# Two mixers of a transformer kernel: gates, branch products and gated sum computed with tokens on the partitions and 512 weight columns streamed

## The chip, the core and the metric

The kernel runs on one core of one Trainium2 chip. The metric is the device time of one execution in microseconds (us); smaller is better. Engines are named as the profile names them: PE is TensorE's matmul, PEld its weight load, DVE is VectorE, ACT is ScalarE, POOL is GpSimd, SP issues the DMAs.

## What is computed

256 tokens of width 1024 pass ten sublayers: two layers of (half a swiglu, first mixer, half a swiglu), then two layers of (second mixer, swiglu). The change touches the ends of the mixers alone, where gated branches are summed and projected:

```python
# first mixer: o_a, o_b, o_c are attention outputs [256, 512]
merged = (sigmoid(ga) * (o_a @ w_br_a)       # ga, gb, gc: [256, 1024] of x @ w_in
          + sigmoid(gb) * (o_b @ w_br_b)     # w_br_*: [512, 1024]
          + sigmoid(gc) * (o_c @ w_br_c))
x = layer_norm(ALPHA * x + merged @ w_out)   # w_out: [1024, 1024]

# second mixer: a [256, 512], conv [256, 256], pooled groups d [256, 4, 64]
merged = g0 * (a @ w_attn_out) + g1 * (conv @ w_conv_out) + g2 * (d @ w_grp) * scale
x = x + merged @ w_o                         # followed by an rmsnorm
```

Sums are to be exact to about float32. Each float32 operand is therefore held as two float32r parts, high and low, and a product is three matmuls: high x high, high x low, low x high.

## The kernel before

Everything stays on chip except the weights. XH and XL (lines 197 and 198) hold the two parts of the transposed input of a sublayer, [128 features, 8 blocks, 256 tokens]. Weights come as slabs of 128 x 1024: `slab` (line 178) loads one by a DMA on SP's queue into one of 4 "raw" buffers, ACT writes its high part `wh` (line 175), DVE its low part `wl` (line 176), each into one of 9 slots. PSUM banks come from four tags (line 156): "acc" 3, "s" 2, "pt" 2, "tp" 1. Pages in SBUF come from tags too (line 155); "gate" and "m" have 2 each.

Two forms of product with x occur. `projects` (line 355) has tokens on the output's partitions: a block of x is the stationary operand, 512 weight columns stream, and it ends with one bank for each tile of 128 tokens (`mm3`, lines 187 to 189). `project_t` (line 369) has features on the output's partitions: a 128 x 128 block of weights is stationary and the 256 tokens stream (`mm3_t`, lines 192 to 194).

The end of a mixer is built of `gates`, `merge`, `branch`, `out_project` (lines 549 to 591), all with features on the partitions. `gates` projects 1024 gate columns in two chunks of 512 through `project_t` and takes tanh(gate / 2) on ACT. `branch` multiplies four feature pairs f2, each [2 x 128 features, 256 tokens] in one "acc" bank, over the K blocks of its weights, and `merge` adds (tanh + 1) * product into the sum M (DVE, lines 561 to 565). `out_project` splits M straight into XH and XL (line 583), loads 8 slabs, and then for each token tile t runs 48 matmuls with 512 columns into two banks and calls `finish(t, O)`. In `finish` (line 885) the result is added to x (lines 299, 300), normed (`layer_norm`, lines 303 to 310, or `rms_norm`, lines 312 to 324), transposed block by block and split into XH and XL for the next sublayer: `to_xt` (line 326) uses the bank "tp" for the first four blocks and "s" (tile 0) or "pt" (tile 1) for the other four.

Nothing in the code orders engines against each other: the framework derives the waits from the tiles, and its scheduler fixes at build time the order of instructions on each engine, by priority of the program's order among what its own model of durations holds for ready. Matmuls of a later part may so be placed into holes of an earlier one: the first gate matmuls stand among the last attention heads.

Of the kernel before, what the change touches and what calls it, by code (L numbers as in the profile page):

```python
# [20 lines left out]
HD = 64  # L21
# [3 lines left out]
# type 1 column groups of w_in  # L25
# [8 lines left out]
# column ranges of the packed constants  # L34
# [39 lines left out]
def slab_cols(w):  # L74
    """[1024, 512 n] -> [n, 4, 128, 2 * 512]: slab (chunk, quarter of K)."""
    n = w.shape[1] // 512
    return w.reshape(4, 2, 128, n, 512).transpose(3, 0, 2, 1, 4).reshape(n, 4, 128, 1024)


def slab_rows(w):  # L80
    """[128 n, 1024] -> [n, 128, 1024]."""
    return w.reshape(-1, 128, 1024)
# [7 lines left out]
def layout(inp):  # L90
    """Data layout only: the arrays as the kernel reads them."""
# [6 lines left out]
    for l in range(DEPTH):  # L98
        for n in ("ffn1", "ffn2"):
# [11 lines left out]
            slab_rows(a["w_br_a"][l]),  # L111
            slab_rows(a["w_br_b"][l].reshape(8, HD, D)[GQA_ORDER].reshape(512, D)),
            slab_rows(a["w_br_c"][l])])
# [6 lines left out]
        o[f"w2_attn_{l}"] = slab_rows(a["w_attn_out_2"][l])  # L120
        o[f"w2_conv_{l}"] = slab_rows(a["w_conv_out_2"][l])
# [22 lines left out]
def block_kernel(ctx: ExitStack, tc: tile.TileContext, I, out, stages=ALL):  # L144
# [28 lines left out]
    def split(dst_h, dst_l, src):  # L173
        """src as the sum of two float32r parts"""
        A.activation(dst_h, src, AF.Copy)  # L175
        V.tensor_sub(dst_l, src, dst_h.bitcast(F32))  # L176
# [103 lines left out]
    def rsqrt(v, n, eps):  # L280
        """(v + eps) ** -0.5"""
# [13 lines left out]
    def add_stats(t, O, c):  # L295
        """X[t] += c * O, with the statistics of the sum"""
# [29 lines left out]
    def to_xt(t, src):  # L326
        """src [128 tokens, 1024] -> the parts of its transpose in XH, XL"""
        for r in range(2):
            p = bank("tp" if r == 0 else ("s", "pt")[t])
            for k in range(4):  # L330
                T.transpose(p[:, k * 128:(k + 1) * 128],
                            src[:, (4 * r + k) * 128:(4 * r + k + 1) * 128], ident)
            sl = (slice(None), slice(4 * r, 4 * r + 4), slice(t * 128, t * 128 + 128))
            split(XH[sl], XL[sl], p.rearrange("p (k n) -> p k n", k=4))

# [19 lines left out]
    def projects(*jobs, ws=None):  # L355
        """x @ [1024, n] for each job (src, evac, n): first token tile of all, then second"""
# [12 lines left out]
    def project_t(src, evac, order=(0, 1, 2, 3)):  # L369
        """(x @ [1024, 512])^T: evac(j, psum) gets feature blocks order[2j], order[2j + 1]"""  # L370
# [86 lines left out]
    def attend(heads, o, vt, vi, pen, mult=None, sinks=None):  # L457
        """heads(h, t, psum): logits of head slot h, tile t. o [128, 2, 8, 64]."""
# [63 lines left out]
    def o_parts(o):  # L522
        """o [128, 2, 8, 64] -> parts of its transpose, [128, 4, 256] each"""
# [10 lines left out]
    def head_transposes(dst, t, src, n=4, scale=None):  # L534
        """src [128, 2n heads, 64] -> dst[:, :n, tile t], two heads on the partitions"""
# [13 lines left out]
    def gates(srcs):  # L549
        gt = [page("gate", [128, 4, S], name="gate") for _ in range(2)]  # L550
        for n in range(2):
            project_t(srcs[n], lambda j, p: A.activation(
                gt[n][:, 2 * j:2 * j + 2], pairs(p), AF.Tanh, scale=0.5))
        return gt

    def merge(gt, f2, p, M, first):
        """M (+)= (tanh(gate / 2) + 1) * p over feature blocks 2 f2, 2 f2 + 1"""
        g = gt[f2 // 2][:, (f2 % 2) * 2:(f2 % 2) * 2 + 2]
        m = M[f2 // 2][:, (f2 % 2) * 2:(f2 % 2) * 2 + 2]
        if first:  # L560
            V.scalar_tensor_tensor(m, g, 1.0, p, op0=OP.add, op1=OP.mult)
        else:
            y = tmp.tile([128, 2, S], F32, tag="ropa", bufs=2, name="gm")
# [3 lines left out]
    def branch(srcs, slabs, parts, M, first):  # L567
        gt = gates(srcs)
        w = [slab(s) for s in slabs]
        for f2 in range(4):  # L570
            p = pairs(bank("acc"))
            for i in range(2):
                c = slice((2 * f2 + i) * 128, (2 * f2 + i) * 128 + 128)
                for k, wk in enumerate(w):
                    mm3_t(p[:, i], (wk[0][:, c], wk[1][:, c]),
                          (parts[0][:, k, :], parts[1][:, k, :]), k == 0, k == len(w) - 1)
            merge(gt, f2, p, M, first)

    def out_project(src, M, finish):
        """finish(t, O) with O = M^T @ [1024, 1024]"""  # L580
        for i in range(4):
            sl = (slice(None), slice(2 * i, 2 * i + 2))
            split(XH[sl], XL[sl], M[i // 2][:, (i % 2) * 2:(i % 2) * 2 + 2])
        w = [slab(src[s]) for s in range(8)]
        for t in range(2):
            O = [bank(("s", "pt")[t]) for _ in range(2)]
# [6 lines left out]
    def new_merged():  # L593
        return [page("m", [128, 4, S], name="merged") for _ in range(2)]

# [1 line left out]
    def mixer1(l, finish):  # L597
        w = I[f"w_in_{l}"]

        def rope(p, t, v, nh):  # L600
            """p [128, nh, 64] rotated, as two terms"""
# [32 lines left out]
        # keys shared by heads: [content, content | index, index | two kv heads]  # L634
# [17 lines left out]
        # indexer scores  # L652
# [30 lines left out]
        # all but the 64 largest scores of a query get the penalty  # L683
# [18 lines left out]
        for i, parts in enumerate((oap, obp, ocp)):  # L702
            branch((w[6 + 2 * i], w[7 + 2 * i]), [I[f"w_br_{l}"][i, s] for s in range(4)], parts,
                   M, i == 0)
# [233 lines left out]
```

## Time and profile before

| | |
|---|---|
| time, median of 3 runs | 2102.02 us (2100.25 to 2103.0) |
| span of the profiled execution | 2109.7 us |
| PE busy | 2067.6 us, 98% |
| DVE busy | 1288.1 us, 61% |
| ACT busy | 944.3 us, 45% |
| DMA | 359.16 MB, mean 170 GB/s |
| mean granted clock of TensorE | 0.993 |

The span runs from the first to the last instruction of one profiled execution; the timed runs are other executions, and their median lies 7.7 us below that span. The share of busy time of PE contains modelled ends of overlapping matmuls; what a matmul costs in a dense stream is read from the distance between the starts of two neighbours in the timeline.

### The profile page before, as it was taken

The page shows a single profiled execution, that of the slowest core. Times are in us where ns is not written, and L with a number is a line of the kernel's source. Part 1 is how long each engine was busy: PE and PEld are TensorE (multiplying, and loading weights), DVE is VectorE, ACT ScalarE, POOL GpSimd, SP SyncE. Part 2 cuts the span into 40 slices and gives each one's busy share as a digit, 9 for nine tenths or more (in the row PEclk, how much of TensorE's full clock was granted, in tenths as well). Part 3 has the DMA queues.
Part 4 walks back from the last instruction along what each step waited for, and adds up shares of the span by engine and source line. Part 5 has one row for each costly group of instructions (what it writes and reads, how often), then busy time and mean ns, then how long its engine had stood idle before and what let it go on. Part 6 is the DMA issues. An engine that isn't in the chain of part 4 may idle for free.

```text
span 2109.7 us, 33644 instructions
## 1 busy us (share of the span) xinstructions
PE 2067.6 (98%) x13656; PEld 1870.0 (89%) x13656; DVE 1288.1 (61%) x2044; ACT 944.3 (45%) x1281; POOL 48.6 (2%) x64
## 2 busy tenths in 40 slices
PE   8999999999999999999999999999999989999999
PEld 7998779988998999788998998789899978997998
DVE  6657974575557555975567557555755565366554
ACT  5543554444444443545435443554344444344442
POOL 0000000000000000000000001200000020000000
PEclk9999999999999999999999999999999999899999
DMA  8654532556555554541556554535565553355552
GB/s 301 197 195 158 173 116 81 180 191 200 188 193 201 178 190 156 178 160 32 170 190 232 183 189 143 181 102 166 181 211 182 175 175 120 112 180 178 192 187 91
DMA packets 99996, 359.16 MB, mean 170 GB/s; under 512 B 11904, under 2 KB 11904, under 8 KB 99840
## 3 DMA queue, kind: packets, MB, share of 16 engines
q1 hardware_dynamic: 99840, 357.00, 50.3%
q8 instruction: 107, 1.75, 0.3%
q14 instruction: 49, 0.40, 0.1%
HBM read 355.91 MB, written 1.05 MB: 169 GB/s over the span
## 4 chain that ended last, share of the span: by engine, by line
PE 87%; DVE 4%; DMA 3%; ACT 2%; POOL 1%; issue 1%; SPq 0%; POOLq 0%; ACTq 0%; DVEq 0%
PE acc L194 16%; PE acc L192 16%; PE acc L193 16%; PE acc L188 4%; PE acc L189 4%; PE acc L187 4%; PE s L187 3%; PE s L188 3%; PE s L189 3%; PE pt L189 3%; PE pt L188 3%; PE pt L187 3%; PE s L627 2%; DVE wl L176 2%; ACT wh L175 2%; PE pt L483 1%
## 5 line engine op out<-in xcount | busy, mean ns | idle before, releaser
L176 DVE TENSOR_TENSOR wl<-raw,wh 128x1024 fp32r<-128x1024 f32 (+1 forms) x656 | 783.8, 1219 | 457.3 <-ACT wh L175 453.5
L175 ACT ACTIVATE wh<-raw 128x1024 fp32r<-128x1024 f32 (+1 forms) x656 | 667.7, 1052 | 487.4 <-PE acc L194 299.6
L192 PE MATMUL acc<-xh,wh 128*128 128x256 f32 x2624 | 745.8, 284 | 0.0
L193 PE MATMUL acc<-xh,wl 128*128 128x256 f32 x2624 | 744.7, 284 | 0.0
L194 PE MATMUL acc<-xl,wh 128*128 128x256 f32 x2624 | 744.5, 284 | 0.0
L192 PEld LDWEIGHTS acc<-xh,wh 128*128 128x128 f32 x2624 | 504.0, 192 | 3.1 <-issue 1.1
L193 PEld LDWEIGHTS acc<-xh,wl 128*128 128x128 f32 x2624 | 504.1, 192 | 1.7
L194 PEld LDWEIGHTS acc<-xl,wh 128*128 128x128 f32 x2624 | 504.1, 192 | 1.5 <-issue 1.5
L187 PE MATMUL acc<-wh,xh 128*128 128x512 f32 (+1 forms) x512 | 203.8, 398 | 7.2 <-ACT wh L175 7.1
L188 PE MATMUL acc<-wl,xh 128*128 128x512 f32 (+1 forms) x512 | 203.0, 396 | 0.5 <-DVE wl L176 0.5
L189 PE MATMUL acc<-wh,xl 128*128 128x512 f32 (+1 forms) x512 | 202.1, 395 | 0.0
L394 DVE SCALAR_TENSOR_TENSOR h<-th,acc 128x256 f32<-128x256 f32 x132 | 55.1, 417 | 169.7 <-ACT th L393 169.7
L393 ACT ACTIVATE th<-acc 128x256 f32<-128x256 f32 x132 | 49.3, 373 | 229.5 <-PE acc L194 201.5
L187 PEld LDWEIGHTS acc<-wh,xh 128*128 128x128 f32 x512 | 98.0, 191 | 27.7 <-ACT wh L175 7.1
L188 PEld LDWEIGHTS acc<-wl,xh 128*128 128x128 f32 x512 | 97.7, 191 | 20.5 <-DVE wl L176 1.5
L189 PEld LDWEIGHTS acc<-wh,xl 128*128 128x128 f32 x512 | 97.4, 190 | 19.5 <-issue 0.7
L187 PE MATMUL s<-wh,ht 128*128 128x512 f32 x264 | 103.5, 392 | 0.0
L188 PE MATMUL s<-wl,ht 128*128 128x512 f32 x264 | 103.4, 392 | 0.0
L189 PE MATMUL pt<-wh,ht 128*128 128x512 f32 x264 | 103.1, 391 | 0.0
L187 PE MATMUL pt<-wh,ht 128*128 128x512 f32 x264 | 103.0, 390 | 0.0
L188 PE MATMUL pt<-wl,ht 128*128 128x512 f32 x264 | 102.8, 389 | 0.0
L189 PE MATMUL s<-wh,ht 128*128 128x512 f32 x264 | 102.0, 389 | 0.0
(249 smaller groups left out, 2246.5 us busy)
## 6 DMA issues: line engine op xcount, KB each, us to landing
raw<-in_w_in_dram SPq DMA_DIRECT2D x184, 512.0 KB, 4.4
raw<-in_ffn_in_dram SPq DMA_DIRECT2D x176, 512.0 KB, 4.6
raw<-in_ffn_out_dram SPq DMA_DIRECT2D x88, 512.0 KB, 4.6
raw<-in_w_ffn_in_dram SPq DMA_DIRECT2D x88, 512.0 KB, 4.4
raw<-in_w_ffn_out_dram SPq DMA_DIRECT2D x44, 512.0 KB, 4.5
raw<-in_w_br_dram SPq DMA_DIRECT2D x24, 512.0 KB, 4.4
raw<-in_w_out_dram SPq DMA_DIRECT2D x16, 512.0 KB, 4.8
raw<-in_w_o_dram SPq DMA_DIRECT2D x16, 512.0 KB, 4.2
```

The source lines that it names most:

```text
L175: A.activation(dst_h, src, AF.Copy)
L176: V.tensor_sub(dst_l, src, dst_h.bitcast(F32))
L187: T.matmul(p, x[0], w[0], start=start, stop=False)
L188: T.matmul(p, x[0], w[1], start=False, stop=False)
L189: T.matmul(p, x[1], w[0], start=False, stop=stop)
L192: T.matmul(p, w[0], x[0], start=start, stop=False)
L193: T.matmul(p, w[1], x[0], start=False, stop=False)
L194: T.matmul(p, w[0], x[1], start=False, stop=stop)
L393: A.activation(th, p[:, :256], AF.Tanh, scale=0.5)
L394: V.scalar_tensor_tensor(h[:, j], th, 1.0, p[:, :256], op0=OP.add, op1=OP.mult)
L483: T.transpose(pt[:, b * 128:b * 128 + 128], sm[:, b * 128:b * 128 + 128], ident)
L627: T.matmul(p, q[b:b + 64, h // 2, t * 128:t * 128 + 128], k[b:b + 64, kslot(h), 0:128 * (t + 1)], start=True, stop=True)
```

## The change

Gates, products and sum get tokens on the partitions. `project_both` replaces `project_t` in `gates`: it fills two "acc" banks at once, one for each token tile, and goes through the K blocks once, with 512 weight columns streamed. The branch weights are laid out anew as two halves of 512 columns with two K blocks in each slab (`slab_halves`); `branch` goes over halves n, then token tiles t, with 512 columns streamed. A page of gates, and a page of the sum, is now [128 tokens, 2 tiles, 512 columns] for each half. The pooling products swap their operands and still stream 256 columns. `out_project` no longer splits the sum straight into XH and XL: for each token tile it first calls `to_xt`, which transposes the sum's eight blocks and splits them; `to_xt` takes a function that gives a block instead of a tensor. The rest of the diff removes comments.

```diff
...
+def slab_halves(w):
+    m = w.shape[0] // 256
+    return w.reshape(m, 2, 128, 2, 512).transpose(3, 0, 2, 1, 4).reshape(2, m, 128, 1024)
...
-            slab_rows(a["w_br_a"][l]),
-            slab_rows(a["w_br_b"][l].reshape(8, HD, D)[GQA_ORDER].reshape(512, D)),
-            slab_rows(a["w_br_c"][l])])
+            slab_halves(a["w_br_a"][l]),
+            slab_halves(a["w_br_b"][l].reshape(8, HD, D)[GQA_ORDER].reshape(512, D)),
+            slab_halves(a["w_br_c"][l])])
         o[f"w_out_{l}"] = slab_rows(a["w_out"][l])
         w = a["w_in_2"][l]
...
         o[f"w2_f_{l}"] = w[:, F2:F2 + 8].reshape(8, 128, 8).transpose(1, 0, 2).reshape(128, 64)
-        o[f"w2_attn_{l}"] = slab_rows(a["w_attn_out_2"][l])
-        o[f"w2_conv_{l}"] = slab_rows(a["w_conv_out_2"][l])
+        o[f"w2_attn_{l}"] = slab_halves(a["w_attn_out_2"][l])
+        o[f"w2_conv_{l}"] = slab_halves(a["w_conv_out_2"][l])
...
     def to_xt(t, src):
         for r in range(2):
             p = bank("tp" if r == 0 else ("s", "pt")[t])
             for k in range(4):
-                T.transpose(p[:, k * 128:(k + 1) * 128],
-                            src[:, (4 * r + k) * 128:(4 * r + k + 1) * 128], ident)
+                T.transpose(p[:, k * 128:(k + 1) * 128], src(4 * r + k), ident)
             sl = (slice(None), slice(4 * r, 4 * r + 4), slice(t * 128, t * 128 + 128))
             split(XH[sl], XL[sl], p.rearrange("p (k n) -> p k n", k=4))
+
+    def blocks(x):
+        return lambda k: x[:, k * 128:k * 128 + 128]
...
+    def project_both(src, evac):
+        w = [slab(src[s]) for s in range(4)]
+        p = [bank("acc") for _ in range(2)]
+        for k in range(8):
+            c = slice((k % 2) * 512, (k % 2) * 512 + 512)
+            for t in range(2):
+                mm3(p[t], xs(k, t), (w[k // 2][0][:, c], w[k // 2][1][:, c]), k == 0, k == 7)
+        flush()
+        for t in range(2):
+            evac(t, p[t])
     def gates(srcs):
-        gt = [page("gate", [128, 4, S], name="gate") for _ in range(2)]
+        gt = [page("gate", [128, 2, 512], name="gate") for _ in range(2)]
         for n in range(2):
-            project_t(srcs[n], lambda j, p: A.activation(
-                gt[n][:, 2 * j:2 * j + 2], pairs(p), AF.Tanh, scale=0.5))
+            project_both(srcs[n], lambda t, p: A.activation(gt[n][:, t], p, AF.Tanh, scale=0.5))
         return gt
 
-    def merge(gt, f2, p, M, first):
-        """M (+)= (tanh(gate / 2) + 1) * p over feature blocks 2 f2, 2 f2 + 1"""
-        g = gt[f2 // 2][:, (f2 % 2) * 2:(f2 % 2) * 2 + 2]
-        m = M[f2 // 2][:, (f2 % 2) * 2:(f2 % 2) * 2 + 2]
+    def merge(g, p, m, first):
         if first:
             V.scalar_tensor_tensor(m, g, 1.0, p, op0=OP.add, op1=OP.mult)
         else:
-            y = tmp.tile([128, 2, S], F32, tag="ropa", bufs=2, name="gm")
+            y = tmp.tile([128, 512], F32, tag="ropa", bufs=2, name="gm")
+            if len(p.shape) == 3:
+                y = y.rearrange("p (a n) -> p a n", a=p.shape[1])
             V.scalar_tensor_tensor(y, g, 1.0, p, op0=OP.add, op1=OP.mult)
             V.tensor_tensor(m, m, y, op=OP.add)
 
     def branch(srcs, slabs, parts, M, first):
         gt = gates(srcs)
-        w = [slab(s) for s in slabs]
-        for f2 in range(4):
-            p = pairs(bank("acc"))
-            for i in range(2):
-                c = slice((2 * f2 + i) * 128, (2 * f2 + i) * 128 + 128)
-                for k, wk in enumerate(w):
-                    mm3_t(p[:, i], (wk[0][:, c], wk[1][:, c]),
-                          (parts[0][:, k, :], parts[1][:, k, :]), k == 0, k == len(w) - 1)
-            merge(gt, f2, p, M, first)
+        for n in range(2):
+            w = [slab(slabs[n, s]) for s in range(slabs.shape[1])]
+            last = 2 * len(w) - 1
+            for t in range(2):
+                p = bank("acc")
+                ts = slice(t * 128, t * 128 + 128)
+                for k in range(last + 1):
+                    c = slice((k % 2) * 512, (k % 2) * 512 + 512)
+                    mm3(p, (parts[0][:, k, ts], parts[1][:, k, ts]),
+                        (w[k // 2][0][:, c], w[k // 2][1][:, c]), k == 0, k == last)
+                merge(gt[n][:, t], p, M[n][:, t], first)
 
     def out_project(src, M, finish):
-        """finish(t, O) with O = M^T @ [1024, 1024]"""
-        for i in range(4):
-            sl = (slice(None), slice(2 * i, 2 * i + 2))
-            split(XH[sl], XL[sl], M[i // 2][:, (i % 2) * 2:(i % 2) * 2 + 2])
         w = [slab(src[s]) for s in range(8)]
         for t in range(2):
+            to_xt(t, lambda k: M[k // 4][:, t, (k % 4) * 128:(k % 4) * 128 + 128])
             O = [bank(("s", "pt")[t]) for _ in range(2)]
             for ks in ((0, 6), (6, 8)) if t == 0 else ((0, 8),):
                 for n, c in enumerate(HALVES):
...
     def new_merged():
-        return [page("m", [128, 4, S], name="merged") for _ in range(2)]
+        return [page("m", [128, 2, 512], name="merged") for _ in range(2)]
...
         for i, parts in enumerate((oap, obp, ocp)):
-            branch((w[6 + 2 * i], w[7 + 2 * i]), [I[f"w_br_{l}"][i, s] for s in range(4)], parts,
-                   M, i == 0)
+            branch((w[6 + 2 * i], w[7 + 2 * i]), I[f"w_br_{l}"][i], parts, M, i == 0)
         out_project(I[f"w_out_{l}"], M, finish)
...
         M = new_merged()
         gt = gates((w[9], w[10]))
-        for f2 in range(4):
-            p = pairs(bank("acc"))
-            n, hb = f2 // 2, f2 % 2
-            r = slice(hb * 64, hb * 64 + 64)
-            for i in range(2):
-                c = slice(n * 256 + i * 128, n * 256 + i * 128 + 128)
-                mm3_t(p[:, i], (pwp[r, 0, c], pwp[r, 1, c]), (ddp[r, 0, n], ddp[r, 1, n]), True, True)
-            merge(gt, f2, p, M, True)
-        branch((w[7], w[8]), [I[f"w2_conv_{l}"][s] for s in range(2)], (cvp[:, 0], cvp[:, 1]),
-               M, False)
-        branch((w[5], w[6]), [I[f"w2_attn_{l}"][s] for s in range(4)], op, M, False)
+        for n in range(2):
+            for hb in range(2):
+                p = pairs(bank("acc"))
+                r = slice(hb * 64, hb * 64 + 64)
+                c = slice(n * 256, n * 256 + 256)
+                for t in range(2):
+                    ts = slice(t * 128, t * 128 + 128)
+                    mm3(p[:, t], (ddp[r, 0, n, ts], ddp[r, 1, n, ts]),
+                        (pwp[r, 0, c], pwp[r, 1, c]), True, True)
+                h = slice(hb * 256, hb * 256 + 256)
+                merge(gt[n][:, :, h], p, M[n][:, :, h], True)
+        branch((w[7], w[8]), I[f"w2_conv_{l}"], (cvp[:, 0], cvp[:, 1]), M, False)
+        branch((w[5], w[6]), I[f"w2_attn_{l}"], op, M, False)
...
         for t in range(2):
-            to_xt(t, rms_norm(t, None, g))
+            to_xt(t, blocks(rms_norm(t, None, g)))
     elif kind0 == "m1":
...
             elif row is not None:
-                to_xt(t, rms_norm(t, mv, rows[-1]))
+                to_xt(t, blocks(rms_norm(t, mv, rows[-1])))
             else:
-                to_xt(t, X[t])
+                to_xt(t, blocks(X[t]))
 
```

## Rows read from the trace of the kernel before

**Rows 1.** The page's head: span, then PE's busy time, share, instructions.

```profile
span 2109.7 us, 33644 instructions
...
PE 2067.6 (98%) x13656; PEld 1870.0 (89%) x13656; DVE 1288.1 (61%) x2044; ACT 944.3 (45%) x1281; POOL 48.6 (2%) x64
```

**Rows 2.** Table by stretch, first mixer's gates and products; busy us (x instructions).

```profile
core 0: us, PE busy (x) PEld busy (x) DVE busy (x) ACT busy (x) POOL busy (x), PEclk, DMA share, GB/s
345.00:440.00 95.00, 95.00 (x795) 95.00 (x794) 51.49 (x55) 40.17 (x49) 0.00 (x0) 1.00 0.54 183
```

**Rows 3.** Timeline of PE, 256 columns; start and duration in us; 56 rows between.

```profile
422.09 0.28 PE L192 MATMUL acc<-xh,wh 128*128 128x256 f32 x1
...
428.93 0.28 PE L192 MATMUL acc<-oh,wh 128*128 128x256 f32 x1
```

**Rows 4.** Timeline of PE: last product, tile 0's 48 matmuls, first of tile 1.

```profile
439.97 0.28 PE L194 MATMUL acc<-ol,wh 128*128 128x256 f32 x1
440.09 0.40 PE L187 MATMUL s<-wh,xh 128*128 128x512 f32 x1
...
451.00 0.39 PE L187 MATMUL pt<-wh,xh 128*128 128x512 f32 x1
```

**Rows 5.** Operations by tile (ns min/median/max, first and last start) and page groups.

```profile
L552 ACT ACTIVATE gate<-acc x48: 572/589/600, 341.5 to 1880.6; 128x512 f32<-128x512 f32 x48
L565 DVE TENSOR_TENSOR merged<-merged,gm x4: 684/692/693, 433.0 to 442.2; 128x512 f32<-128x512 f32 x4
L176 DVE TENSOR_TENSOR wl<-raw,wh 128x1024 fp32r<-128x1024 f32 (+1 forms) x656 | 783.8, 1219 | 457.3 <-ACT wh L175 453.5
L175 ACT ACTIVATE wh<-raw 128x1024 fp32r<-128x1024 f32 (+1 forms) x656 | 667.7, 1052 | 487.4 <-PE acc L194 299.6
```

**Rows 6.** Timelines of DVE, PE, ACT: end of the first mixer, layer 0.

```profile
451.20 0.69 DVE L299 SCALAR_TENSOR_TENSOR x<-s,x 128x512 f32<-128x512 f32 x1
454.78 1.42 DVE L310 SCALAR_TENSOR_TENSOR x<-x,rsr,lnrow 128x512 f32<-128x512 f32 x2 [0.46 <-POOL rsr L285]
455.58 0.66 PE L331 MATMUL tp<-k,x 128*128 128x128 f32 x4 [0.57 <-DVE x L310]
456.00 0.48 PE L189 MATMUL pt<-wh,xl 128*128 128x512 f32 x1
456.34 0.60 ACT L175 ACTIVATE xh<-tp 128x512 fp32r<-128x512 f32 x1 [12.22 <-PE tp L331]
456.97 0.69 DVE L176 TENSOR_TENSOR xl<-tp,xh 128x512 fp32r<-128x512 f32 x1 [0.77 <-ACT xh L175]
463.58 0.39 PE L187 MATMUL acc<-wh,xh 128*128 128x512 f32 x1
```

**Rows 7.** The same for the second mixer, layer 0, and its gain row's DMA issues.

```profile
1496.93 0.39 PE L187 MATMUL pt<-wh,xh 128*128 128x512 f32 x1
1500.87 0.66 PE L331 MATMUL tp<-k,h 128*128 128x128 f32 x4 [0.84 <-DVE h L323]
1502.26 0.69 DVE L176 TENSOR_TENSOR xl<-tp,xh 128x512 fp32r<-128x512 f32 x1 [0.78 <-ACT xh L175]
1509.78 0.39 PE L187 MATMUL acc<-wh,xh 128*128 128x512 f32 x1
lnrow<-in_rms_g_dram SPq DMA_DIRECT2D x2, 512.0 KB, 4.3
```

**Rows 8.** Timelines of DVE and PE, second mixer, layer 1: users of bank "tp".

```profile
1737.41 0.69 DVE L723 TENSOR_TENSOR qs<-qs,rsr 128x512 f32<-128x512 f32 x1 [1.88 <-POOL rsr L285]
1738.02 0.17 DVE L758 COPY z<-tp 128x16 f32<-128x16 f32 x1
1740.73 0.59 PE L768 MATMUL tp<-k,lf 128*8 128x256 f32 x2 [1.72 <-DVE lf L766]
1743.66 0.60 PE L538 MATMUL tp<-k,qs 128*128 128x128 f32 x4
```

**Rows 9.** Timeline of PE around a hole, then the stretch of lower granted clock.

```profile
1301.05 0.39 PE L189 MATMUL pt<-wh,ht 128*128 128x512 f32 x1
1303.32 0.78 PE L331 MATMUL tp<-k,h 128*128 128x128 f32 x4 [1.88 <-DVE h L323]
...
1303.66:1307.08 3.42, 3.42 (x12) 2.58 (x11) 2.87 (x6) 2.14 (x3) 0.00 (x0) 0.50 0.10 42
```

## The prediction

> **What bounds the kernel now.** I read the head of the page first: TensorE is at work for 98% of the span [rows 1]. That number alone says little, because the ends of matmuls are modelled, so the second view is the table by stretch for the stage that the change rewrites, gates and branch products of the first mixer [rows 2]: TensorE is busy through all of its 95 us, with 795 matmuls, while VectorE works for 54% and ScalarE for 42%. The third view is the timeline of single matmuls. Where they follow each other without a hole, the step from one start to the next is the cost. 57 steps with 256 columns take 428.93 - 422.09 = 6.84 us, 120.0 ns each [rows 3]; 48 steps with 512 columns take 451.00 - 440.09 = 10.91 us, 227.3 ns each [rows 4]. So the stage is bound by the number and width of its matmuls. The fourth view is the end of a mixer, where TensorE waits for other engines [rows 6, 7]. There the change is dearer than its few instructions suggest.
>
> **The change, part by part.** *Wider streaming.* One 512-column matmul replaces two of 256 columns and saves 2 x 120.0 - 227.3 = 12.7 ns. The pairs, from the code: a gate chunk has 96 matmuls now and 48 after, a product with K = 512 likewise, conv (K = 256) 48 and 24; pooling keeps 24 of 256 columns. The first mixer has 6 chunks and 3 products, 9 x 48 = 432 pairs; the second 6 chunks, one product and conv, 7 x 48 + 24 = 360. Both run twice: 1584 pairs, 20.1 us. All of it lies on the path, since nothing else limits that stage [rows 2].
>
> Here the Trainium skill speaks against the change: "TensorE: Matmul & The Clock Gate", Back-to-back issue gap, gives 262 cycles for 256 columns and 518 for 512, so that at 2.4 GHz a pair would save only 2.5 ns, 4 us in all (an estimate from that page). The trace does not agree: its step is 120.0 ns, not 109, and the rows decide.
>
> *What moves without a price.* Weight slabs, tanh, merges and splits keep their number and sizes. A slab is given back after its 12 matmuls (2.7 us) instead of being held until the last feature block, so loading gets easier. One place is tighter: two of three "acc" banks are now filled at once. The next chunk wants the first of them 3 + 3 matmuls, 1.36 us, after its last matmul; the tanh needs 0.2 to start plus 0.59 [rows 5]. If ScalarE has just begun a weight conversion of 1.05 us [rows 5], TensorE waits 0.5 us. That can happen at 12 places; I take 0 and keep 0 to 6.
>
> *The front of the last projection, 4 times.* Before, the sum has features on the partitions, is split straight into XH and XL while the last products run, and the projection starts one step after the last product (439.97, 440.09) [rows 4]. After, eight transposes stand between. Four transposes lead to the end of their XL split in 2.08 us (455.58 to 456.97 + 0.69) [rows 6], and the third matmul needs XL. But VectorE first has the last merge, two operations of 0.69 [rows 5] from about 0.2 on, so XL comes at 2.3 instead of 2.1; two matmuls (0.45) run meanwhile: 1.9 us lost. If a weight split of 1.22 [rows 5] has just started, 2.7. I take the middle, 2.3, four times 9.2 us (7.6 to 10.8).
>
> *The second token tile, 4 times: the dear part.* `out_project` now calls `to_xt(1, ...)` after `finish(0, ...)`. Both want the bank "tp", of which there is one (line 156). The program asks for it in the order: sum tile 0, normed tile 0 (inside `finish(0)`), sum tile 1. I take it that the bank is handed out in the order of the program. A place of the second mixer supports this: "tp" is free from 1738.19, the queries' last transposes, later in the program, have their input at 1738.10, yet the next to use "tp" is the running sum at 1740.73, earlier in the program, and those transposes come at 1743.66 [rows 8]. It is no proof, since TensorE's order is fixed at build time. Then the second tile's first four blocks wait until tile 0 has been summed, normed, transposed and split. In the first mixer that ends, counted from the end of tile 0's matmuls at 451.00, at 457.66 = +6.66 [rows 6]; another pass of transposes and splits takes 2.08, with 0.1 for the handover: the third matmul of tile 1 starts at +8.8, two have run: 8.35 lost. Already before, tile 1 took 463.58 - 451.00 = 12.58 for 10.91 of matmuls [rows 4, 6], 1.67 lost, so +6.7. In that hole the scheduler can place the next stage's matmuls on its one loaded slab (6 x 0.227 = 1.36; I take 1.3): 5.4. In the second mixer the norm is shorter: +6.02, then 2.08 and 0.1, less 0.45, is 7.75; before it lost 12.85 - 10.91 = 1.94 [rows 7]; 5.8 less 1.3 is 4.5. Sum 2 x 5.4 + 2 x 4.5 = 19.8 us; without the filling 25.0.
>
> *Clock.* TensorE now stands idle for 4 us or more in each mixer. After the hole from 1301.05 to 1303.32 the granted clock was 0.5, the lower level of 1.2 GHz, for 3.42 us [rows 9]. A full stretch under dense matmuls costs 1.7 us; part will fall on waiting. Bounds 0 and 3.4 (two stretches) for each mixer; I take 1.2, 4.8 in all.
>
> *A row that waits.* The next norm's gain row lands in a page of tag "m", which the sum now holds longer. Its load takes 4.3 us [rows 7]. If the second tile's other four transposes (bank "pt") run during tile 0's matmuls, the page is free in time: 0. If they run only after, the row comes about 2 us late in the second mixer. I take 0, bound 0 to 4 for the two.
>
> *Sum:* 9.2 + 19.8 + 4.8 - 20.1 = +13.7 us. Against the profiled execution: 2109.7 becomes 2123.4. The median of the timed runs is 2102.02, 7.7 below that span; I carry the difference over: 2115.7. With low prices (7.6, 19.8, no clock loss) it is +7.3, 2109.3; with all high ones (10.8, 25.0, 13.6, 4, 6) +39, 2141. That all come together is unlikely; I go to 2128.
>
> **The rivals.** *B, the bank goes to whoever is ready first.* Then tile 1's transposes run right after tile 0's matmuls, and only its XL split waits behind `finish(0)` on VectorE. In the first mixer VectorE is taken from 451.20 until the norm's end at 456.2, with one short hole [rows 6]; the third matmul comes at +4.0 (split in the hole) or +5.9. Less 0.45, less the 1.67 of before, plus 0.8 for `finish(0)`'s transposes: 2.7 to 4.6, say 3.6. In the second mixer VectorE has a hole for the root from +2.1: 2.8 - 0.45 - 1.94 + 0.8 = 1.2. Then 2 x 3.6 + 2 x 1.2 = 9.6 in place of 19.8 and no clock loss: 9.2 + 9.6 - 20.1 = -1.3, 2100.7. Against it stands [rows 8].
>
> *C, faster: the tail hides.* If tile 1's transposes and splits all run during tile 0's 10.9 us of matmuls, and tile 0's among the last products, the price is TensorE's time for 64 transposes alone: four hold it about 0.42 (456.00 - 455.58) [rows 6], 16 x 0.42 = 6.7; 6.7 - 20.1 = -13.4, 2088.6. It decides whether tile 1's XL is written before tile 0's last matmul. For it: VectorE and ScalarE have time there. Against it: one "tp" bank, and transposes that stand behind tile 0's matmuls in the program.
>
> *D, the pair saves nothing.* The new matmuls alternate every three between two banks, which no run of 512-column matmuls here does as a whole. If a step took 240 ns, the change would not do what it says: 9.2 + 19.8 + 4.8 = +33.8, 2135.8. Against it: the steps in [rows 4] are as long in either bank order that the trace has.
>
> By the Trainium skill's figure above the sum would be +29.8, 2131.8, near rival D.
>
> **How the numbers follow.** Forecast 0.80; B 0.10; C 0.06; D 0.04. Predicted: 2115.7. The range goes from 2099 to 2128: it takes in most of B below, and the forecast with dear clock, no filling and a late row above; C, D and the ends are left out. A measurement of this kernel can tell about 0.2% (4.2 us) from no change. Faster by more: C and a little of B, 0.09. Within: the rest of B and the forecast's low end, 0.09. Slower: 0.82.
>
> **What would show it.** Right: steps of about 227 ns through gates and products; then, at each mixer's end, tile 1's first four transposes only after the XL split of `finish(0)`, with TensorE idle 4 us or more after tile 0's last matmul and some 8.8 us (8.2 in the second mixer) until tile 1's third matmul, and a stretch at clock 0.5 near it. Tile 1's transposes ahead of `finish(0)`'s would be B, both ahead of tile 0's end C; steps near 240 ns D. I would be wrong if the scheduler found other work for the hole, or if gates moved into attention changed its length by several us.

## Result: 1.1% slower, and the profile after

The changed kernel takes 2127.09 us (median; 2123.68 to 2128.95) against 2101.22 (2100.25 to 2103.0) for the kernel before in the same series: a ratio of 1.0114, 95% interval 1.0094 to 1.0133, 25.9 us more. The forecast was 2115.7 in a range of 2099 to 2128: the direction and the mechanisms came out, the size did not (13.7 us forecast). The median lies only 0.9 us inside the upper end of the range, and two of its four runs (2128.2 and 2128.95) lie above it: that the range held is in part luck.

The line numbers of the changed kernel: matmuls L193 to L195, `split` L181 (high part) and L182 (low part), `to_xt`'s transposes L337, `merge` L584 and L585, the addition to x L305. The head of the page after, the counterpart of [rows 1]: TensorE has less work, 1520 matmuls less, and the span is longer.

```profile
span 2124.2 us, 30622 instructions
...
PE 2061.5 (97%) x12136; PEld 1789.9 (84%) x12136; DVE 1293.8 (61%) x2044; ACT 953.3 (45%) x1281; POOL 47.5 (2%) x64
```

TensorE's timeline through gates and products of the first mixer, layer 0 (start and duration in us), the counterpart of [rows 3]. From the first to the second row there are 278 steps without a hole: 63.04 us, 226.8 ns each, in gates and products alike.

```profile
373.54 0.39 PE L193 MATMUL acc<-wh,xh 128*128 128x512 f32 x1
...
436.58 0.40 PE L195 MATMUL acc<-wh,ol 128*128 128x512 f32 x1
```

The front of the last projection, timeline of TensorE, VectorE and ScalarE; before, the projection started one step after the last product [rows 4].

```profile
435.64 1.07 ACT L181 ACTIVATE wh<-raw 128x1024 fp32r<-128x1024 f32 x1 [3.02 <-PE acc L195]
...
436.58 0.40 PE L195 MATMUL acc<-wh,ol 128*128 128x512 f32 x1
436.74 1.23 DVE L182 TENSOR_TENSOR wl<-raw,wh 128x1024 fp32r<-128x1024 f32 x1 [0.56 <-ACT wh L181]
436.81 0.60 PE L337 MATMUL tp<-k,merged 128*128 128x128 f32 x4
437.01 1.06 ACT L181 ACTIVATE wh<-raw 128x1024 fp32r<-128x1024 f32 x1 [0.30 <-PE acc L195]
437.25 0.60 PE L337 MATMUL s<-k,merged 128*128 128x128 f32 x4
437.89 0.68 DVE L584 SCALAR_TENSOR_TENSOR gm<-gate,acc 128x512 f32<-128x512 f32 x1
...
438.48 1.22 DVE L182 TENSOR_TENSOR wl<-raw,wh 128x1024 fp32r<-128x1024 f32 x1
438.61 0.53 PE L193 MATMUL s<-wh,xh 128*128 128x512 f32 x1 [0.76 <-ACT xh L181]
...
439.62 0.69 DVE L585 TENSOR_TENSOR merged<-merged,gm 128x512 f32<-128x512 f32 x1
440.22 0.69 DVE L182 TENSOR_TENSOR xl<-tp,xh 128x512 fp32r<-128x512 f32 x1
440.36 0.66 PE L337 MATMUL pt<-k,merged 128*128 128x128 f32 x4 [0.99 <-DVE merged L585]
...
440.96 0.51 PE L195 MATMUL s<-wh,xl 128*128 128x512 f32 x1
```

The last product leaves its place at 436.81; two matmuls run, and the third, which needs XL, comes at 440.96: 440.96 - 436.81 - 0.45 = 3.70 us lost. It is 3.70 in each of the four mixers. VectorE is the late one, and it isn't late with the sum's own work: two splits of weights, 1.23 and 1.22 us, stand in its queue, one ahead of the last merge and one between the merge's two operations. Their slots came free just then: ScalarE's first conversion waited 3.02 us for a product to end. The last merge isn't needed by this XL either: it is tile 1's, and tile 1's transposes wait for it (440.36); it stands ahead in the same queue.

The second token tile, timeline of the same mixer, the counterpart of [rows 6].

```profile
450.39 0.69 DVE L305 SCALAR_TENSOR_TENSOR x<-s,x 128x512 f32<-128x512 f32 x1 [8.02 <-PE s L195]
...
451.32 0.39 PE L195 MATMUL s<-wh,xl 128*128 128x512 f32 x1
...
456.13 0.92 PE L337 MATMUL tp<-k,x 128*128 128x128 f32 x4 [4.42 <-DVE x L316]
456.85 1.06 PE L337 MATMUL s<-k,x 128*128 128x128 f32 x4
...
457.72 0.69 DVE L182 TENSOR_TENSOR xl<-tp,xh 128x512 fp32r<-128x512 f32 x1 [0.98 <-ACT xh L181]
...
458.76 1.05 PE L337 MATMUL tp<-k,merged 128*128 128x128 f32 x4
...
460.48 0.69 DVE L182 TENSOR_TENSOR xl<-tp,xh 128x512 fp32r<-128x512 f32 x1 [1.22 <-ACT xh L181]
460.62 0.39 PE L193 MATMUL pt<-wh,xh 128*128 128x512 f32 x1
...
461.31 0.41 PE L195 MATMUL pt<-wh,xl 128*128 128x512 f32 x1
```

Tile 0's last matmul ends its step at 451.55. The bank "tp" goes to the normed tile 0 first (456.13); when its XL split is done at 458.41, the sum of tile 1 gets it (458.76). The hole before 456.13 is idle for 4.42 us. The table by stretch shows the clock there (columns as in [rows 2]): the lower level for one stretch, and four transposes take 0.92 to 1.06 us where they take 0.60 in the front.

```profile
core 0: us, PE busy (x) PEld busy (x) DVE busy (x) ACT busy (x) POOL busy (x), PEclk, DMA share, GB/s
...
456.38:459.79 3.41, 3.41 (x15) 2.69 (x14) 1.74 (x3) 1.20 (x2) 0.00 (x0) 0.50 0.02 5
```

From the end of tile 0's matmuls to the end of tile 1's the four mixers now take 19.99, 21.33, 19.47 and 19.34 us; before it was 12.58, 12.61, 12.85 and 12.84 [rows 4, 6, 7]. A part comes back, because matmuls of the next sublayer run in the hole.

### The profile page after: what moved, and what is told of

It is laid out like the page before. It is cut to its first block, busy times and chain, and to the rows that moved or that the text cites. A ratio compares the mean times of both kernels' runs of the same rounds, so it can differ in the third digit from the quotient of the medians.

```text
span 2124.2 us, 30622 instructions
## 1 busy us (share of the span) xinstructions
PE 2061.5 (97%) x12136; PEld 1789.9 (84%) x12136; DVE 1293.8 (61%) x2044; ACT 953.3 (45%) x1281; POOL 47.5 (2%) x64
## 5 line engine op out<-in xcount | busy, mean ns | idle before, releaser
L182 DVE TENSOR_TENSOR wl<-raw,wh 128x1024 fp32r<-128x1024 f32 (+1 forms) x656 | 790.5, 1221 | 446.0 <-ACT wh L181 442.0
L181 ACT ACTIVATE wh<-raw 128x1024 fp32r<-128x1024 f32 (+1 forms) x656 | 675.4, 1054 | 556.7 <-PE acc L200 187.9
L198 PE MATMUL acc<-xh,wh 128*128 128x256 f32 x1856 | 525.9, 283 | 0.0
L199 PE MATMUL acc<-xh,wl 128*128 128x256 f32 x1856 | 525.6, 283 | 0.0
L200 PE MATMUL acc<-xl,wh 128*128 128x256 f32 x1856 | 525.2, 283 | 0.0
L193 PE MATMUL acc<-wh,xh 128*128 128x512 f32 (+1 forms) x896 | 357.4, 400 | 6.2 <-ACT wh L181 6.1
L199 PEld LDWEIGHTS acc<-xh,wl 128*128 128x128 f32 x1856 | 356.1, 192 | 1.7
L198 PEld LDWEIGHTS acc<-xh,wh 128*128 128x128 f32 x1856 | 356.0, 192 | 1.7
L194 PE MATMUL acc<-wl,xh 128*128 128x512 f32 (+1 forms) x896 | 355.2, 396 | 0.9 <-DVE wl L182 0.9
L200 PEld LDWEIGHTS acc<-xl,wh 128*128 128x128 f32 x1856 | 356.0, 192 | 0.0
L195 PE MATMUL acc<-wh,xl 128*128 128x512 f32 (+1 forms) x896 | 354.9, 396 | 0.0
L193 PEld LDWEIGHTS acc<-wh,xh 128*128 128x128 f32 x896 | 171.6, 191 | 43.3 <-ACT wh L181 6.5
L195 PEld LDWEIGHTS acc<-wh,xl 128*128 128x128 f32 x896 | 170.6, 190 | 34.5 <-issue 1.1
L401 ACT ACTIVATE th<-acc 128x256 f32<-128x256 f32 x132 | 49.2, 373 | 227.9 <-PE acc L200 202.0
L193 PE MATMUL s<-wh,ht 128*128 128x512 f32 x264 | 103.4, 392 | 0.0
L195 PE MATMUL pt<-wh,ht 128*128 128x512 f32 x264 | 103.1, 391 | 0.0
L193 PE MATMUL pt<-wh,ht 128*128 128x512 f32 x264 | 103.0, 390 | 0.0
L195 PE MATMUL s<-wh,ht 128*128 128x512 f32 x264 | 101.9, 389 | 0.0
```

The lines of the kernel that those rows point to most:

```text
L193: T.matmul(p, x[0], w[0], start=start, stop=False)
L194: T.matmul(p, x[0], w[1], start=False, stop=False)
L195: T.matmul(p, x[1], w[0], start=False, stop=stop)
L198: T.matmul(p, w[0], x[0], start=start, stop=False)
L199: T.matmul(p, w[1], x[0], start=False, stop=False)
L200: T.matmul(p, w[0], x[1], start=False, stop=stop)
```

## Experiments

**The wide streaming alone.** `e4_no_sum` takes the way of the sum out:

```diff
         for t in range(2):
-            to_xt(t, lambda k: M[k // 4][:, t, (k % 4) * 128:(k % 4) * 128 + 128])
             O = [bank(("s", "pt")[t]) for _ in range(2)]
```

> Left out: the transposes and splits of the gated sum; the last projection multiplies what XH and XL still hold. Gates, branch products and merges are as in the changed kernel. It shows the saving of the wide streaming alone. Theory (12.7 ns a pair, 1584 pairs): 2101.2 - 20.1 = 2081; the attention stretch of the two first mixers was 1.3 and 0.9 us longer, so 2083 (2079 to 2087). By the step that the Trainium skill's page gives (2.5 ns a pair) it would be 2097. If wide streaming saved nothing: 2101.

Measured: 2081.12 us (2079.14 to 2096.76), ratio to before 0.9901 [0.9863, 0.9938]. That is 20.1 us under 2101.22, or 20.8 by the ratio (13 to 29 by its interval). The projection follows the last product at the next step:

```profile
435.84 0.39 PE L195 MATMUL acc<-wh,ol 128*128 128x512 f32 x1
436.06 0.39 PE L193 MATMUL s<-wh,xh 128*128 128x512 f32 x1
```

So a pair does save 12.7 ns or a little more (2 x 120.0 - 226.8 = 13.2), and rival D is out. The Trainium skill's step ("TensorE: Matmul & The Clock Gate", Back-to-back issue gap), by which this kernel would have taken 2097 (an estimate from that page), doesn't agree with the measured 2081: its 4 us lie outside the interval. The run also gives the price of the sum's way in the changed kernel: 2127.1 - 2081.1 = 46.0 us, where the forecast had 9.2 + 19.8 + 4.8 = 33.8. The whole error is in that price.

**Is it the bank or the place in the program?** Two kernels that each change one of the two. `e1_order` keeps the bank and moves the call:

```diff
-        for t in range(2):
-            to_xt(t, lambda k: M[k // 4][:, t, (k % 4) * 128:(k % 4) * 128 + 128])
+        def sum_xt(t):
+            to_xt(t, lambda k: M[k // 4][:, t, (k % 4) * 128:(k % 4) * 128 + 128])
+
+        sum_xt(0)
+        for t in range(2):
             O = [bank(("s", "pt")[t]) for _ in range(2)]
...
+            if t == 0:
+                sum_xt(1)
             finish(t, O)
```

> The sum's second token tile is transposed in program order ahead of finish(0) instead of behind it; nothing else differs from the changed kernel (2127.1 us). Theory (one bank, handed out in the order of the program): the second tile's first four transposes now follow tile 0's last matmul at once. Only its splits still share VectorE with finish(0), as in my rival B: 3.6 us for each first mixer and 1.2 for each second, 9.6 in all, where the four stages with the tails are 25.6 us longer than before in the two profiles. That is 16 us less: 2111 (2106 to 2116), and the stretches at clock 0.5 at the mixers' ends go. Rival (VectorE's order decides, not the bank): the split of the second tile stays behind finish(0) and under 4 us are won: 2123 to 2127.

Measured: 2104.1 us (2101.17 to 2107.14), ratio to before 0.9996 [0.9976, 1.0017]. 23 us are won, more than the 16 expected, and the time lies under the expected 2106 to 2116. The timeline at the end of tile 0:

```profile
449.98 0.39 PE L195 MATMUL s<-wh,xl 128*128 128x512 f32 x1
450.21 0.60 PE L337 MATMUL tp<-k,merged 128*128 128x128 f32 x4
...
451.14 0.69 DVE L306 BATCH_NORM_STATS2 st<-x 128x6 f32<-128x512 f32 x1
...
451.75 0.67 DVE L182 TENSOR_TENSOR xl<-tp,xh 128x512 fp32r<-128x512 f32 x1
```

The transposes stand right behind tile 0's last matmul, and the XL split stands in the middle of `finish(0)`'s work, behind the additions to x and their statistics and ahead of the norm. From tile 0's end to tile 1's end it takes 13.79, 13.79, 14.05 and 14.06 us: 1.2 more than before in all four. My rival B had 1.2 for the second mixer and 3.6 for the first; for the first I had let the split wait at least for the hole within the norm (third matmul at +4.0), and the order on VectorE has it ahead of the norm (third matmul at 452.53, +2.3). The forecast had the stretches at clock 0.5 go. Those of the tails went, but in three of the four mixers one now follows the front's wait (from 437.89, 1086.43 and 1881.73), and tile 0 takes 1.4 to 1.6 us longer there.

`e2_bank` keeps the place in the program and gives the second tile another bank:

```diff
-    def to_xt(t, src):
+    def to_xt(t, src, tag="tp"):
...
-            p = bank("tp" if r == 0 else ("s", "pt")[t])
+            p = bank(tag if r == 0 else ("s", "pt")[t])
...
-            to_xt(t, lambda k: M[k // 4][:, t, (k % 4) * 128:(k % 4) * 128 + 128])
+            to_xt(t, lambda k: M[k // 4][:, t, (k % 4) * 128:(k % 4) * 128 + 128],
+                  "tp" if t == 0 else "acc")
```

> The program's order stays as in the changed kernel (second tile behind finish(0)), but the second tile's first four transposes get an acc bank instead of the one tp bank. Theory (the single bank is the cause, the order matters only because of it): with a bank of their own the transposes and splits of tile 1 move into tile 0's matmuls; the 25.6 us of the four tails go, less up to 0.6 us each for transposes that now run in front: 2127.1 - 25.6 + 0 to 2.4 = 2102 to 2104, bounds 2099 to 2107. Rival (the place in the program behind finish(0) decides, whichever bank): no change, 2124 to 2129.

Measured: 2097.28 us (2095.12 to 2100.81), ratio 0.9976 [0.996, 0.9991]. 29.8 us are won, and the time lies under the bounds of 2099 to 2107: by the profiles the four stages that follow a mixer are 28 us shorter than in the changed kernel, where 25.6 were expected. Timeline of the front and of the end of tile 0:

```profile
435.59 0.60 PE L337 MATMUL acc<-k,merged 128*128 128x128 f32 x4
...
438.68 0.48 PE L193 MATMUL pt<-wh,xh 128*128 128x512 f32 x1
...
439.32 0.68 DVE L182 TENSOR_TENSOR xl<-acc,xh 128x512 fp32r<-128x512 f32 x1
...
449.20 0.39 PE L195 MATMUL s<-wh,xl 128*128 128x512 f32 x1
449.43 0.39 PE L194 MATMUL pt<-wl,xh 128*128 128x512 f32 x1
```

Tile 1's transposes now run in the hole of the front, even its first matmul does (438.68), and tile 1 follows tile 0 at the next step. From tile 0's end it takes 12.38, 12.35, 12.63 and 12.61 us, 0.2 less than before. So the place behind `finish(0)` does no harm by itself: the hole comes from two users of one bank that is handed out in the order of the program, and either a bank more or an earlier place removes it. The rival to each of the two experiments falls.

**What makes the front so dear?** `e3_hold` holds back the conversion of two slabs, the projection's last and the next sublayer's first, by a small write ahead of each that reads XL. The first write waits for the sum's XL. The second stands in the program behind `finish(0)`, which writes XL anew, and so waits for that:

```diff
+        if held:
+            held.pop()
+            A.activation(wh[0:1, 0:4], XL[0:1, 7, 0:4].bitcast(F32), AF.Copy)
         split(wh[:, :n], wl[:, :n], raw[:, :n])
...
-        w = [slab(src[s]) for s in range(8)]
+        w = [slab(src[s]) for s in range(7)]
         for t in range(2):
             to_xt(t, lambda k: M[k // 4][:, t, (k % 4) * 128:(k % 4) * 128 + 128])
+            if t == 0:
+                held.extend((1, 1))
+                w.append(slab(src[7]))
```

> As the changed kernel, but two weight slabs (the last of the projection, the first of the next sublayer) are converted only after the first tile's XL has been written: a small write that reads XL stands before their conversion. The front (from the last product's end until the projection runs densely) took 3.8 us in three mixers and 5.35 in the fourth, where I had forecast 2.3. Theory: two weight splits of 1.22 us that VectorE runs ahead of the last merge and of XL make up the difference; without them the front takes 1.9 to 2.3, 1.5 to 1.9 us less in each mixer: 2127.1 - 6 to 7.6 = 2119.5 to 2121. Rival: the front is set by ScalarE and the transposes themselves, 2125 to 2128. Rival: the late slabs are missed by the next sublayer in the hole of the second tile, slower, up to 2131.

Measured: 2123.95 us (2121.55 to 2135.26), ratio to before 1.0115 [1.0083, 1.0146]: 3.1 us less than the changed kernel by the medians, which the spread of both hardly tells from nothing. The front itself and the end of its hole, VectorE, TensorE and ScalarE (in this kernel the matmuls are L198 to L200, the transposes L342, the merge L589 and L590, the small write L193):

```profile
434.26 0.39 PE L200 MATMUL acc<-wh,ol 128*128 128x512 f32 x1
...
434.69 0.69 DVE L589 SCALAR_TENSOR_TENSOR gm<-gate,acc 128x512 f32<-128x512 f32 x1 [0.82 <-PE acc L200]
...
435.41 0.69 DVE L590 TENSOR_TENSOR merged<-merged,gm 128x512 f32<-128x512 f32 x1
...
436.02 0.68 DVE L182 TENSOR_TENSOR xl<-tp,xh 128x512 fp32r<-128x512 f32 x1
...
436.76 0.50 PE L200 MATMUL s<-wh,xl 128*128 128x512 f32 x1
...
454.52 0.69 DVE L182 TENSOR_TENSOR xl<-s,xh 128x512 fp32r<-128x512 f32 x1 [0.16 <-ACT xh L181]
...
456.06 0.19 ACT L193 ACTIVATE wh<-xl 1x4 fp32r<-1x4 f32 x1
...
456.28 1.06 ACT L181 ACTIVATE wh<-raw 128x1024 fp32r<-128x1024 f32 x1
```

The weight splits are gone from it, and it loses 436.76 - 434.49 - 0.45 = 1.82 us, in each of the four mixers, instead of 3.70. That is the low end of my forecast (1.9), and the two conversions, with their splits, are shown to cost 1.88 us each time, 7.5 in all. The time didn't follow, since the rival with the late slab holds too: the next sublayer's first slab is converted only at 456.28 (last row), behind the small write at 456.06 that had to wait for `finish(0)`'s XL, so nothing can fill the hole of the second tile. The granted clock then stays at 0.50 for 10.24 us (from 451.82) and in the other three tails for 6.83, where the changed kernel has 3.41, once 6.83. From tile 0's end to tile 1's end it takes 22.67, 21.06, 20.59 and 20.45 us, 4.6 us more in the sum of the four than in the changed kernel; the whole stages that follow a mixer, with the work that had filled the hole, are 9.0 us longer by the profiles. The edit so shows the front's price, and its own side effect takes the gain back.

**The front hidden by another order.** `e5_front` lets the last branch finish tile 0 for both halves first and puts its transposes there:

```diff
...
+        ws = {}
+        for a in range(2):
+            for b in range(2):
+                n, t = (b, a) if final else (a, b)
...
                 merge(gt[n][:, t], p, M[n][:, t], first)
+            if final and a == 0:
+                sum_xt(M, 0)
...
```

> Only the front is changed: the last branch goes over the token tiles in the outer loop, so that tile 0's sum is ready 24 matmuls (5.4 us) before the last product, and its transposes stand between them. The second tile is left behind finish(0). Theory: the front's 3.70 us of waiting in each mixer are hidden and only eight transposes of TensorE's own time stay, 2 x 0.44: 2127.1 - 4 x (3.70 - 0.88) = 2115.8 (2113 to 2119). Rival: the four slabs that the last branch now holds to its end come free later, the projection waits for its own slabs, and under 4 us are won: 2123 to 2130.

Measured: 2117.37 us (2113.81 to 2126.98); the ratio to before, 1.0053 [1.0028, 1.0078], is against a series in which the kernel before had a median of 2107.8 (the last experiment says why), so the time stands better against 2127.1: 9.7 us won, 11.3 expected. The projection starts one step after the last product in all four mixers, 3.70 becomes 0. Timelines of the front (first mixer, layer 0) and of the second tile (second mixer, layer 0):

```profile
435.31 0.39 PE L195 MATMUL acc<-wh,ol 128*128 128x512 f32 x1
435.53 0.39 PE L193 MATMUL s<-wh,xh 128*128 128x512 f32 x1
...
1497.09 0.60 PE L337 MATMUL pt<-k,merged 128*128 128x128 f32 x4
...
1501.52 1.41 DVE L329 SCALAR_TENSOR_TENSOR h<-x,rsr,lnrow 128x512 f32<-128x512 f32 x2 [1.86 <-DMA lnrow<-in_rms_g_dram]
```

The second tile costs 0.9 us more on average than in the changed kernel (20.50, 21.18, 20.65 and 21.53 us from tile 0's end to tile 1's end), most of it in the second mixers. Tile 1's other four transposes (bank "pt"), which ran in the front's hole, now stand behind tile 0's last matmul in all four mixers (1497.09). So their XL split falls among `finish(0)`'s work, and in the second mixers the page that the gain row wants comes free late: VectorE stands idle for 1.86 us until the row has landed, and for 1.74 in layer 1, where in the changed kernel it stood idle for 1.01 behind GpSimd's root. That is the forecast's row that waits, here in another kernel. In the last mixer the stretch at clock 0.50 is also longer, 6.83 us (from 1902.07) for 3.41. What each of these is worth was not separated.

**Both together.** `e6_both` is `e5_front` with the second tile's call moved ahead of tile 0's last quarter of matmuls (against `e5_front`):

```diff
-            if t == 1:
-                sum_xt(M, 1)
...
             for ks in ((0, 6), (6, 8)) if t == 0 else ((0, 8),):
+                if ks == (6, 8):
+                    sum_xt(M, 1)
```

> e5_front's order of the last branch, and the second tile's transposes in program order after three quarters of tile 0's matmuls, ahead of finish(0); the bank tp stays the only one of its kind. Theory: nothing of the way back to features on the partitions is waited for any more, only the transposes' own time on TensorE is left, 64 of them, 16 x 0.44 = 7.0 us over the kernel without transposes (2081.1): 2088 (2085 to 2092), which is my rival C by another way; 0.7% faster than before. Rival: TensorE waits at one of the two new places for a merge or a split on VectorE, 1 to 2 us each time: 2092 to 2100.

Measured: 2089.29 us (2086.88 to 2090.13), ratio to before 0.992 [0.9894, 0.9947]: faster than both kernels (0.6% by the median against 2101.2; its slowest run, 2090.1, lies under the fastest of the kernel before in any series, 2098.5). The timeline around tile 1's transposes and around the change of tiles:

```profile
443.29 0.39 PE L195 MATMUL s<-wh,xl 128*128 128x512 f32 x1
443.52 0.60 PE L337 MATMUL tp<-k,merged 128*128 128x128 f32 x4
443.95 0.60 PE L337 MATMUL pt<-k,merged 128*128 128x128 f32 x4
444.31 0.48 PE L193 MATMUL s<-wh,xh 128*128 128x512 f32 x1
...
446.90 0.39 PE L195 MATMUL s<-wh,xl 128*128 128x512 f32 x1
447.13 0.39 PE L193 MATMUL pt<-wh,xh 128*128 128x512 f32 x1
```

No engine is waited for at either place: eight transposes take 444.31 - 443.52 = 0.79 us, and tile 1 follows tile 0. The four mixers need 12.59, 12.57, 12.83 and 12.85 us from tile 0's end to tile 1's end, as before. What is left of the sum's way is 2089.3 - 2081.1 = 8.2 us against 7.0 expected; the transposes' own time is 8 x 0.79 = 6.3 of it, the rest was not followed. That is the state of my rival C, with nearly its time (2088.6); the change as it stands is not in it, because neither tile's transposes have a place with cover.

**Was the profile of before a usual execution?** `e0_before` is the kernel before, unchanged.

> The kernel before once more, unchanged, for another profiled execution. In the profile on which the prediction rests the granted clock was 0.5 for 20.48 us inside the attention of the last mixer, and its span was 2109.7 where the timed runs lie near 2101. Theory: that stretch belongs to that one execution; this profile has none there, its span is 2097 to 2103, and the last mixer's stage takes about 200.5 us instead of 210.87. Rival: the stretch comes in every execution; the span is near 2109.7 again.

Measured: 2110.27 us, span 2108.5. Neither expectation holds as it stood. The stretch is not where it was: the last mixer's stage takes 202.0 us here, 210.9 there (from the first addition to x at the end of one sublayer to that of the next). But the mixer before it has one of the same length, again in attention; tables by stretch (columns as in [rows 2]), first of the execution on which the prediction rests, then of this one:

```profile
1784.94:1805.42 20.48, 20.48 (x82) 17.19 (x83) 4.76 (x22) 5.81 (x14) 0.00 (x0) 0.50 0.09 26
...
1385.96:1406.44 20.48, 20.48 (x81) 16.76 (x80) 5.34 (x24) 6.23 (x15) 0.00 (x0) 0.50 0.09 28
```

That stage takes 212.1 us instead of 204.5. So such a stretch costs some 7.6 to 8.9 us (the execution on which the prediction rests has a short stretch of 3.41 us more in either stage, which lowers the one figure and raises the other), and it comes in some executions of the kernel before and not in others: in the series of these three kernels its times (2099.9 to 2121.4) lie for the most part in groups near 2101, 2109 and 2120, and the mean granted clock of these runs falls with them: 0.998 to 0.999, 0.993 to 0.995, 0.988 to 0.989. All four runs of it in the result lie in the first group, so the 25.9 us are counted against executions without such a stretch. The profiles of the changed kernel and of the six made from it show none. Their times say a little more: one of the six runs of `e4_no_sum` took 2096.76 us at a mean clock of 0.993, the others 2079.1 to 2081.7 at 0.998 to 1.0: 15.6 us over the median, twice the price of one such stretch, though no profile shows what that run did. What starts it can't be told from these profiles.

## Why the prediction was right, and where it was short

| term | forecast | measured |
|---|---|---|
| wide streaming | -20.1 | -20.1 (`e4_no_sum` against 2101.2; interval -29 to -13) |
| front, four times | +9.2 | +14.8 (4 x 3.70) |
| second tile, with clock | +24.6 | +26.1 (the four stages after a mixer, changed kernel less `e4_no_sum`) |
| clock in the first tile | in the above | +1.5 (one mixer) |
| not followed | 0 | +3.6 (by the same stages: 0.5 in the sublayers ahead of the first mixers, 1.6 in the mixers; the rest between profiles and medians) |
| sum | +13.7 | +25.9 |

*Bound and wide streaming: right.* The stage is bound by matmuls, and their step is 226.8 ns after as it was 227.3 before. The handover of the "acc" banks was rightly taken at 0: 278 steps stand in one row without a hole, and 256 ahead of the last product in the second mixers.

*The front: right in mechanism, mis-sized, and the largest miss.* The term that failed is 2.3 us for the wait for XL. The working had VectorE's last merge and, as the dear end, one weight split of 1.22 that has just begun. There are two, and the fault was to treat them as chance: a weight slot comes free exactly when the last products end, so conversions are due at that moment every time, in the same place of a queue that is fixed at build time. The prediction's "a slab is given back after its 12 matmuls" holds for the gates alone: a branch uses each slab for both token tiles, so its last two come free six matmuls before the end and with the last one, and there the two conversions start (435.64 and 437.01). It shows as 3.70 four times over, and `e3_hold` takes 1.88 of it away. The price with both in it, and nothing else changed, is 3.7, a full microsecond above the dear end.

*The second tile: right.* Tile 1 waits for the bank until `finish(0)`'s split, as [rows 8] suggested, and `e1_order` and `e2_bank` show both halves of the reason. The first matmul on XL came 461.31 - 451.55 = 9.8 us after tile 0's end, not 8.8 (11.1 in layer 1, and 9.3 and 9.1 in the second mixers, not 8.2): the lower clock fell upon the transposes, which I had priced at full clock and then charged as a separate 1.2. Together the two terms were 24.6 forecast, 26.1 measured.

*Clock: right in kind.* Each tail now has its stretch at 0.50, one of double length (6.83 us from 1108.32). The one that I hadn't thought of stands behind the front's wait in the second mixer, layer 0, at 1497.44: the first tile takes 12.11 us from its third matmul on, 10.59 in the others. The same wait was followed by such a stretch in three of four mixers of `e1_order` and in none of `e2_bank` (3.83 us of wait there), so one profile of each kernel doesn't tell where it comes.

*The gain row: right.* It is asked for at 1497.69 in the second mixer, layer 0, and used at 1512.80 without a wait for it. The other case, a row asked for after tile 0's matmuls and waited for, came up in `e5_front`.

*The base: a hidden flaw.* The profile of before held a half-clock stretch worth 7.6 to 8.9 us that the timed runs did not. Carrying the 7.7 us over to the forecast was therefore sound, as the sum doesn't touch that stretch. But the two profiles by themselves mislead: their spans differ by 14.5 us, as if the sum of 13.7 had been exact, while the times differ by 25.9. [rows 9] were read for the price of a short stretch; the long one stood in the same execution's table by stretch, and I passed over it.

*The rivals.* B and C both fell for the kernel as it is, and both came up as kernels: `e1_order` is B's state, `e6_both` C's. D fell with the step.

## What to carry to other kernels

Before pricing a step that runs at the end of a stage, list what else becomes due at that moment on its engine: buffers that are given back there bring their refills with them, in every pass and not by chance. A single buffer that the program hands out in its written order makes the order of two calls a dependency; look for the place where the second call is written, and write it ahead of the work that can cover it. When a stage is made cheaper by a layout that needs a transposition, put the transposition among matmuls that don't depend on it: here that made 46 us of price into 8.

## What the hardware showed

Besides stretches of 3.41 us at the lower granted clock that follow a hole of TensorE, there is one of 20.48 us that begins without one. In both executions it lies in the attention of a second mixer, in the eight microseconds ahead of it no two starts on TensorE lie more than 0.61 us apart, and the DMA share within it is 0.09. A step of 1.20 us ends 8.5 and 8.0 us ahead of it, but a step of 1.20 us stands at the same place of the other second mixer's attention in both executions, and one of 1.27 in both of the changed kernel's (1391.25 and 1792.67), and no such stretch follows there. One such stretch moves this kernel's time by 0.4%, twice what its measurement otherwise resolves, so one profile next to a median of other executions should be searched for it first. What starts it stayed open.
